# An MLP in Winograd's seven products: sums at set times, operands kept in DRAM, Silu in one step, and the last two pairs in eight products

## The chip, the cores and the metric

The kernel runs on one core of a Trainium2 chip. The metric is the device time of one execution in microseconds (us), as the median of several runs. Beside it stands one execution taken with a profile, with its own time and its span, the time from the first to the last instruction. Engines: PE is TensorE (PEld its weight loads), DVE is VectorE, ACT is ScalarE, POOL is GpSimd, SP is SyncE, which here issues the DMAs.

## The reference

The reference is one layer of a hybrid decoder trunk on x of 2048 rows by 1024 columns in float32: an RMS norm and an input projection, three mixers side by side (a diagonal state space model, a sparse attention, a gated linear recurrence), an output projection with residual, and then the part that this change is about, which ends with the final norm:

```python
h = h + mix @ w_out[l]
h = h + swiglu(rmsnorm(h, norm_ffn[l]), w_gate[l], w_up[l], w_down[l])
return rmsnorm(h, norm_final)

def swiglu(h, w_gate, w_up, w_down):
    return (jax.nn.silu(h @ w_gate) * (h @ w_up)) @ w_down
```

w_gate and w_up are 1024 by 2816, w_down is 2816 by 1024.

## The kernel before

The program has three stages. phase_a does the projections and phase_b the mixers and the output projection; it leaves the 16 tiles of 128 rows in DRAM as hS and their sums of squares in ssq. The change touches phase_c, the MLP, only.

**The MLP.** The 2048 rows are taken in two halves (s = 0 and 1) of 1024. In each half the product of weights and normalised rows is done by Winograd's form of Strassen's method: a two by two product in seven products instead of eight, with sums ahead of them and behind them. The 22 tiles of 128 columns of the hidden layer go in 11 pairs (fp). pair does, for the gate (j = 0) and the up matrix (j = 1), the seven products of a pair. Their weight operands are sums S1 to S4 of the raw weights (make, tiles "S", four buffers), split by part into a rounded high part "ah" and a low remainder "al" in float32r. Their row operands B11, B21, T2, T1, T3, B22 and T4 are 512 by 512 blocks of the rows and of differences of them, transposed by TensorE in turn4 and split into high and low as well. A product of high and low parts leaves out low by low, so each is 12 matmuls of 512 columns (4 steps of 128 by 3). The products' results are summed on VectorE and POOL to the four blocks of a pair; silu and give then make silu(gate) * up, and give writes this block and Winograd's sums of it to DRAM (gS, products 1 to 7). silu is Tanh on ScalarE and then th + 1 times g on VectorE (twice the Silu; give halves it).

**The down product.** After its 11 pairs a half does down, again by seven products, in groups of one or two pairs (GROUPS_D, six groups). fetch loads an operand pair of a product, high from gS and low from w_down or wS (its sums) through "raw", rounds it on ScalarE and takes the remainder on VectorE or POOL. block multiplies it and adds the result in PSUM (tiles "P", six banks) to one of 28 accumulators M[k, t] in SBUF, whose buffers are those of S, U2, th and other tiles of the pairs (ACC_TAGS). In the last group combine adds the accumulators up to the four blocks of the output, squares are summed on ScalarE, and finish takes a root and scales: by a VectorE step with the gain, or by a ScalarE step and a POOL multiplication. In the second half the last group has its row tile t as the outer loop, so that finish can follow each t.

**Rows and weight sums.** rows_a and rows_b make the row operands of the first half. The normalised rows of T2, T1 and T3 are made from rows loaded early into h5, l5, h6 and l6, which B22 and T4 need as their own place later; the differences overwrite the rows, so a second round of rows_b loads the rows from hS again, scales them by gain and makes the differences for B22 and T4. down_sums makes one pair's sums of w_down (wS), and ahead the second half's rows and differences (tS, four sets). Both use the tile "nx", three buffers, and "t3", one.

**The order.** Nothing here is ordered by hand on an engine. Plan records every operation with a key and, if floor is set, an earliest time, and then goes through time: a free engine takes the ready operation with the lowest key. The times of operations are the planner's own costs. What comes out is the fixed order of each engine's queue. A tile with n buffers waits for the n-th tile before it of the same name, in the order of the program:

```python
r = self.rings.setdefault(ring, [])
r.append(ref)
ref.old += r[-1 - bufs:-bufs]
```

Keys run with planned TensorE time: a product takes STEP_C, 2.724, a pair 14 of them, and the pairs of the first half end at x = 419.5. Weight parts have a key 12 ahead of their product (LEAD_W), raw weights 40, fetches of the down product 24.

## Time and profile before

| | us |
|---|---|
| median of 3 runs | 2781.14 |
| lowest and highest of them | 2781.03, 2782.69 |
| the profiled execution | 2778.5 |
| its span | 2776.7 |

| engine | busy us | share of the span |
|---|---|---|
| PE | 2577.2 | 93% |
| PEld | 2095.7 | 75% |
| DVE | 2296.8 | 83% |
| ACT | 1352.3 | 49% |
| POOL | 1376.6 | 50% |

The mean granted clock of TensorE was 0.966 of full speed. Times in the rows below count from the start of the span. phase_c lies between about 1390 us and the end. Nearly all its instructions are recorded by one helper and so carry one line, L207; they are told apart by their tiles. Busy shares are means over stages with different limits, so they are read stage by stage.

### The profile page before, as it was taken

The page shows a single profiled execution, that of the slowest core. Times are in us where ns is not written, and L with a number is a line of the kernel's source. Part 1 is how long each engine was busy: PE and PEld are TensorE (multiplying, and loading weights), DVE is VectorE, ACT ScalarE, POOL GpSimd, SP SyncE. Part 2 cuts the span into 40 slices and gives each one's busy share as a digit, 9 for nine tenths or more (in the row PEclk, how much of TensorE's full clock was granted, in tenths as well). Part 3 has the DMA queues.
Part 4 walks back from the last instruction along what each step waited for, and adds up shares of the span by engine and source line. Part 5 has one row for each costly group of instructions (what it writes and reads, how often), then busy time and mean ns, then how long its engine had stood idle before and what let it go on. Part 6 is the DMA issues. An engine that isn't in the chain of part 4 may idle for free. (4 is left out here: it accounts for less than half of the span.)

```text
span 2776.7 us, 43054 instructions
## 1 busy us (share of the span) xinstructions
PE 2577.2 (93%) x14889; PEld 2095.7 (75%) x14889; DVE 2296.8 (83%) x4480; ACT 1352.3 (49%) x2820; POOL 1376.6 (50%) x971
## 2 busy tenths in 40 slices
PE   6988889989999999998969989999998999999996
PEld 5756568777887788877758777887886888888785
DVE  8797776259898999999899999878889887877877
ACT  5662433147877777876633323344345333334433
POOL 2445441124544343443266766665466555556446
PEclk9999999979999999999989999999999999999998
DMA  5455556662212121121436665346654233326652
GB/s 170 121 157 161 148 137 199 204 171 61 70 41 64 36 64 41 41 52 41 143 105 227 242 228 198 113 145 239 214 180 148 107 107 113 104 90 235 218 200 82
DMA packets 231706, 376.11 MB, mean 135 GB/s; under 512 B 67040, under 2 KB 114912, under 8 KB 231488
## 3 DMA queue, kind: packets, MB, share of 16 engines
q1 hardware_dynamic: 185456, 339.27, 37.6%
q0 software_dynamic: 43872, 26.22, 4.7%
q10 hardware_dynamic: 2160, 7.87, 0.7%
q8 instruction: 118, 1.93, 0.3%
q14 instruction: 100, 0.82, 0.1%
HBM read 259.84 MB, written 113.44 MB: 134 GB/s over the span
## 5 line engine op out<-in xcount | busy, mean ns | idle before, releaser
L207 PE MATMUL B<-h,al 128*128 128x512 f32 x1232 | 486.7, 395 | 16.7 <-POOL al L207 11.2
L207 PE MATMUL B<-h,ah 128*128 128x512 f32 x1232 | 485.8, 395 | 16.7 <-ACT ah L207 7.1
L207 PE MATMUL B<-l,ah 128*128 128x512 f32 x1232 | 485.0, 394 | 4.5 <-DVE l L207 4.5
L207 PE MATMUL B<-l,h 128*128 128x512 f32 x1848 | 431.6, 394 | 11.7 <-POOL l L207 5.3
L207 PEld LDWEIGHTS B<-l,h 128*128 128x128 f32 x1848 | 348.0, 190 | 88.7 <-POOL l L207 8.2
L207 PEld LDWEIGHTS B<-h,al 128*128 128x128 f32 x1232 | 233.7, 190 | 72.4 <-POOL al L207 15.3
L207 PEld LDWEIGHTS B<-h,ah 128*128 128x128 f32 x1232 | 234.2, 190 | 67.0 <-ACT ah L207 8.2
L207 POOL TENSOR_TENSOR l<-raw,l 128x1024 fp32r<-128x1024 f32 (+1 forms) x84 | 195.8, 2342 | 170.2 <-ACT l L207 144.8
L207 PEld LDWEIGHTS B<-l,ah 128*128 128x128 f32 x1232 | 234.1, 190 | 54.7 <-DVE l L207 6.2
L393 DVE SCALAR_TENSOR_TENSOR ptl<-B,pth 128x512 f16<-128x512 f32 (+3 forms) x408 | 246.1, 624 | 22.4 <-ACT pth L384 21.1
L384 ACT ACTIVATE pth<-B 128x512 f16<-128x512 f32 (+3 forms) x408 | 214.4, 548 | 55.9 <-PE B L1509 31.6
L399 PE MATMUL B<-wo,mix 128*128 128x512 f32 x768 | 227.0, 412 | 4.7 <-DMA mix<-mixS 3.9
L207 ACT ACTIVATE ah<-S 128x512 fp32r<-128x512 f32 x176 | 110.4, 628 | 236.2 <-PE B L207 183.6
L207 POOL TENSOR_TENSOR U<-U,s 128x512 f32<-128x512 f32 x96 | 151.8, 1581 | 102.4 <-DVE U L207 57.3
L207 POOL TENSOR_TENSOR al<-S,ah 128x512 fp32r<-128x512 f32 x92 | 149.0, 1620 | 94.8 <-ACT ah L207 94.8
L384 ACT ACTIVATE Ps<-Ps,mn 128x1024 f32<-128x1024 f32 (+7 forms) x192 | 172.7, 902 | 41.3 <-DVE mn L1412 40.1
L399 PE MATMUL B<-KB,Q 128*128 128x384 f32 (+3 forms) x448 | 185.1, 413 | 6.4 <-DVE im L396 2.1
L207 PE MATMUL B<-hnl,wsh 128*128 128x512 f32 x448 | 183.3, 409 | 1.8 <-DVE hnl L207 1.8
L207 PE MATMUL B<-hnh,wsh 128*128 128x512 f32 x448 | 182.6, 408 | 0.5 <-ACT stage L207 0.3
L1509 PE MATMUL B<-ident,Ps 128*128 128x128 f32 x1088 | 181.1, 277 | 1.2 <-ACT Ps L384 0.8
L207 PE MATMUL B<-hnh,wsl 128*128 128x512 f32 x448 | 179.2, 400 | 0.0
L399 PE MATMUL B<-VV,ptl 128*128 128x64 f16 x1448 | 148.2, 195 | 27.8 <-DVE ptl L393 26.8
(371 smaller groups left out, 6282.1 us busy)
## 6 DMA issues: line engine op xcount, KB each, us to landing
raw<-in_wgu SPq DMA_DIRECT2D x88, 512.0 KB, 3.7
raw<-gS SPq DMA_DIRECT2D x70, 512.0 KB, 3.9
gS<-U SPq DMA_DIRECT2D x88, 256.0 KB, 2.1
raw<-wS SPq DMA_DIRECT2D x40, 512.0 KB, 4.0
gS<-s SPq DMA_DIRECT2D x66, 256.0 KB, 2.1
raw<-in_wd SPq DMA_DIRECT2D x66, 256.0 KB, 3.8
wraw<-in_wzf SPq DMA_DIRECT2D x28, 512.0 KB, 4.4
nx<-in_x SPq DMA_DIRECT2D x24, 512.0 KB, 4.5
```

Source lines behind the costliest of these rows:

```text
L207: f(*[real(x) for x in a], **{n: real(x) for n, x in k.items()})
L384: return self.S.activation(o, i, f, **k)
L393: return (eng or self.V).scalar_tensor_tensor(o, a, s, b, op0=op0, op1=op1, **k)
L399: return self.PE.matmul(o, l, r, start=start, stop=stop)
L1509: self.PE.transpose(pt.v[:, j - a], P.v[:, c:c + 128], self.ident)
```

## The change

Six things change, all in phase_c.

- **B22 and T4 by DRAM.** rows_b runs once. It stores b1 (B22) to the new uT, makes the differences for T2 and T4 together, stores b0 (T4) too, and transposes T2, T1 and T3; T3 lies in an "nx" tile. rows_c, from time 10 on, loads both blocks back and transposes them.
- **Silu.** silu is one ScalarE step with the function Silu in place; give multiplies gate and up in a plain product.
- **Earliest times.** down_sums of pair fp gets the floor 70 + 25 fp and the key 80 + 25 fp (before: 13 and 50 + 33 fp). ahead of set j gets the floor x - 190 + 25 j with x = 419.5, its key x - 150 + 25 j as before.
- **The last two pairs of the second half in eight products.** give keeps only the block itself for pairs 9 and 10 (eS) and makes no sums of it. down does five groups by seven products and combines after the fifth; ends then does, for each of the 8 row tiles and both column halves, the plain product of the last two pairs (12 matmuls each, over their four blocks of 128 hidden columns), adds it to the combined accumulator, and finish follows after the tiles two by two and one by one at the end. combine's sums into 3 go from POOL to VectorE, in both halves.
- **finish.** The first column half of the first half's tiles is scaled and multiplied by the gain in one VectorE step, instead of ScalarE and POOL; the second half's tiles, but the last, use that step for both column halves. LAST, the tiles whose gain is multiplied in before the root, is 15 alone.
- **The planner** knows Silu as a table of its own.

```diff
 GROUPS_D = (1, 2, 2, 2, 2, 2)
+TAIL = 9
...
 FIRST = ((0, 1), (1, 2), (2, 3), (3, 4))
-LAST = (11, 15)
+LAST = (15,)
...
-TABLE = {AF.Exp: 0, AF.Tanh: 0, AF.Sqrt: 1, AF.Sin: 2}
+TABLE = {AF.Exp: 0, AF.Tanh: 0, AF.Sqrt: 1, AF.Sin: 2, AF.Silu: 3}
...
         self.wS = {k: [d(f"wS{k}_{g}", [128, n, 512]) for g, n in enumerate(GROUPS_D)] for k in (4, 5, 6, 7)}
+        self.eS = d("eS", [2, 2, 128, 2, 512])
+        self.uT = [d(f"uT{j}", [2, 128, 512]) for j in range(4)]
...
                 pool.tile([128, n], F32, name=name, bufs=bufs)
-            self.recorded(pool, psum, BANKS_C, ("rstd", "ssq", "hS", "gS", "wS", "tS"), self.mlp, START_C)
+            self.recorded(pool, psum, BANKS_C, ("rstd", "ssq", "hS", "gS", "eS", "wS", "tS", "uT"), self.mlp, START_C)
...
-        def rows_b(j, names):
+        def rows_b(j):
             if j == 0:
-                for n in names:
+                for n in ("T2", "T1", "T3"):
                     operand(0, n)
-            if "T2" in names:
-                x0 = early[j // 2][:, j % 2]
-                x1 = row(4 + j, early[2 + j // 2][:, j % 2])
-                t3 = x1[:, 512:]
-            else:
-                x1, x0 = row(4 + j), row(j)
-                t3 = pool.tile([128, 512], F32, name="t3", bufs=1)
+            x0 = early[j // 2][:, j % 2]
+            x1 = row(4 + j, early[2 + j // 2][:, j % 2])
+            t3 = pool.tile([128, D], F32, name="nx", bufs=3)[:, :512]
             a0, b0, a1, b1 = x0[:, :512], x0[:, 512:], x1[:, :512], x1[:, 512:]
-            differences(a0, b0, a1, b1, t3, names)
-            src = {"T3": t3, "B22": b1, "T2": a0, "T1": a1, "T4": b0}
-            for n in names:
-                turn4(src[n], ops[0, n], 128 * j)
+            self.dma(self.uT[j][0], b1)
+            differences(a0, b0, a1, b1, t3, ("T2", "T4"))
+            self.dma(self.uT[j][1], b0)
+            for n, x in (("T2", a0), ("T1", a1), ("T3", t3)):
+                turn4(x, ops[0, n], 128 * j)
+        def rows_c(j):
+            if j == 0:
+                for n in ("B22", "T4"):
+                    operand(0, n)
+            x = pool.tile([128, D], F32, name="nx", bufs=3)
+            self.dma(x.rearrange("p (a b) -> p a b", a=2), self.uT[j].rearrange("a p b -> p a b"))
+            for i, n in enumerate(("B22", "T4")):
+                turn4(x[:, 512 * i:512 * i + 512], ops[0, n], 128 * j)
...
         def silu(g):
-            th = small("th")
-            self.act(th, g, AF.Tanh, scale=0.5)
-            self.stt(g, th, 1.0, g, OP.add, OP.mult)
+            self.act(g, g, AF.Silu)
...
             keep = lambda k, x: self.dma(self.gS[s][k][gi][:, j], x)
-            self.stt(g, g, 0.5, u, OP.mult, OP.mult)
+            self.tt(g, g, u, OP.mult)
+            if s and fp >= TAIL:
+                self.dma(self.eS[c][fp - TAIL][:, r], g)
+                return
...
-            n, first, r = GROUPS_D[gi], sum(GROUPS_D[:gi]), []
+            n, first, r = 2 if k is None else GROUPS_D[gi], sum(GROUPS_D[:gi]), []
...
                 raw = pool.tile([128, KT, 128], F32, name="raw", bufs=4).rearrange("p a b -> p (a b)")[:, :512 * n]
-                if tag == "h" or k in self.wS:
+                if k is None:
+                    src = self.eS[gi // 2][gi % 2].rearrange("p a b -> p (a b)") if tag == "h" else io["wd"][2 * TAIL + gi]
+                    self.at(x - LEAD_G, 0, self.dma, raw, src)
+                elif tag == "h" or k in self.wS:
...
                 tt(6, 1)
-                tt(3, 6, G)
+                tt(3, 6)
             elif k == 5:
-                tt(3, 5, G)
+                tt(3, 5)
...
                 tt(7, 5)
-            i = 8 * s + t
-            for i, dh, o, after in ((i, 0, 2, 2), (i, 1, 3, 3), (i + 4, 0, 4, 4), (i + 4, 1, 7, 7)):
-                if k == after:
-                    a, d = M[o, t], slice(512 * dh, 512 * dh + 512)
-                    acc[i, dh] = a
-                    junk = pool.tile([128, 512], BF, name="junk", bufs=1)
-                    self.at(x + .3, 0, lambda: self.act(junk, a, AF.Square, accum_out=ms[:, dh, col(i):col(i) + 1]))
-                    if i in LAST:
-                        if i not in last:
-                            last[i] = pool.tile([128, D], F32, name="nx", bufs=3)
-                        self.at(x + .3, 0, self.tt, last[i][:, d], a, gfin[dh], OP.mult, self.G if dh else None)
+            for i, dh, o in ((t, 0, 2), (t, 1, 3), (4 + t, 0, 4), (4 + t, 1, 7)):
+                if k == o and not s:
+                    squares(i, dh, M[o, t], x)
+        def squares(i, dh, a, x):
+            acc[i, dh], d = a, slice(512 * dh, 512 * dh + 512)
+            junk = pool.tile([128, 512], BF, name="junk", bufs=1)
+            self.at(x + .3, 0, lambda: self.act(junk, a, AF.Square, accum_out=ms[:, dh, i:i + 1]))
+            if i in LAST:
+                if i not in last:
+                    last[i] = pool.tile([128, D], F32, name="nx", bufs=3)
+                self.at(x + .3, 0, self.tt, last[i][:, d], a, gfin[dh], OP.mult)
+        def ends(i, dh, hw, x):
+            c, t = i // 4, i % 4
+            a, d = M[{(0, 0): 2, (0, 1): 3, (1, 0): 4, (1, 1): 7}[c, dh], t], slice(512 * dh, 512 * dh + 512)
+            ps = psum.tile([128, 512], F32, name="P")
+            def products():
+                for r in range(4):
+                    g, w = hw[2 * c + r // 2][0][:, :, 512 * (r % 2) + 128 * t:512 * (r % 2) + 128 * t + 128], hw[r][1][:, :, d]
+                    self.mm(ps, g[:, 0], w[:, 0], r == 0, False)
+                    self.mm(ps, g[:, 0], w[:, 1], False, False)
+                    self.mm(ps, g[:, 1], w[:, 0], False, r == 3)
+            self.at(x, 0, products)
+            self.at(x + 2.724, 0, self.tt, a, a, ps, OP.add)
+            squares(8 + i, dh, a, x + 2.724)
...
             totals(s, x)
-            for gi, n in enumerate(GROUPS_D):
-                end = gi == len(GROUPS_D) - 1
-                u = .681 * n
-                at = lambda p, t: x + u * (7 * t + p if end and s else 4 * p + t)
-                hw = {k: fetch(s, k, gi, p, at(p, 0)) for p, k in enumerate(seq)}
-                for t, p in ((t, p) for t in range(4) for p in range(7)) if end and s else ((t, p) for p in range(7) for t in range(4)):
-                    k, y = seq[p], at(p, t)
+            groups = GROUPS_D[:-1] if s else GROUPS_D
+            for gi, n in enumerate(groups):
+                u, end = .681 * n, gi == len(groups) - 1
+                hw = {k: fetch(s, k, gi, p, x + 4 * u * p) for p, k in enumerate(seq)}
+                for p, t in ((p, t) for p in range(7) for t in range(4)):
+                    k, y = seq[p], x + u * (4 * p + t)
...
                         combine(s, t, k, y + u)
-                        if s and k == 4:
-                            self.at(y + u + 1, 0, finish, 8 + t, 12 + t)
-                        elif not s and t == 3 and k in (3, 4):
+                        if not s and t == 3 and k in (3, 4):
...
                 x += 28 * u
+            if s:
+                hw = [fetch(s, None, r, r, x) for r in range(4)]
+                for i in range(8):
+                    for dh in range(2):
+                        ends(i, dh, hw, x)
+                        x += 2.724
+                    if i in (1, 3, 5):
+                        self.at(x + 1, .01, finish, 7 + i, 8 + i)
+                    elif i > 5:
+                        self.at(x + 1, 0, finish, 8 + i)
...
         M = {}
-        col = lambda i: i if i < 8 else 8 + 2 * (i % 4) + (i - 8) // 4
...
             n = len(tiles)
-            c = col(tiles[0])
+            c = tiles[0]
...
                         a = acc[i, dh]
-                        if i > 7 and dh == 0:
+                        if i > 7 or dh == 0:
...
                     self.at(x - 50 + j, 0, rows_a, j)
-                for n, names in enumerate((("T2", "T1", "T3"), ("B22", "T4"))):
-                    plan.floor = 10.0 if n else -100.0
-                    for j in range(4):
-                        self.at(x - 6 + 18 * n + 3 * j, 0, rows_b, j, names)
+                for j in range(4):
+                    self.at(x - 6 + 3 * j, 0, rows_b, j)
+                plan.floor = 10.0
+                for j in range(4):
+                    self.at(x + 12 + 3 * j, 0, rows_c, j)
...
                 if s == 0:
-                    self.at(50 + 33 * fp, 0, down_sums, fp)
+                    plan.floor = 70.0 + 25 * fp
+                    self.at(80 + 25 * fp, 0, down_sums, fp)
+                    plan.floor = REST_C
...
                 for j in range(4):
+                    plan.floor = x - 190 + 25 * j
                     self.at(x - 150 + 25 * j, 0, ahead, j)
+                plan.floor = REST_C
...
```

## Rows read from the trace of the kernel before

**Rows 1.** Windows of phase_c; columns: engines' busy us (instructions), granted clock, DMA share, GB/s

```profile
core 0: us, PE busy (x) PEld busy (x) DVE busy (x) ACT busy (x) POOL busy (x), PEclk, DMA share, GB/s
1430.00:1460.00 30.00, 19.17 (x78) 14.09 (x77) 28.60 (x31) 7.25 (x13) 17.86 (x12) 0.83 0.52 164
1570.00:1610.00 40.00, 36.59 (x160) 29.31 (x159) 36.32 (x39) 12.42 (x22) 30.19 (x20) 1.00 0.69 237
1610.00:1697.00 87.00, 76.05 (x311) 59.12 (x310) 82.15 (x80) 22.84 (x41) 58.69 (x36) 0.96 0.67 225
2080.00:2130.00 50.00, 38.53 (x176) 29.40 (x175) 46.68 (x69) 30.23 (x63) 31.01 (x21) 0.86 0.37 124
2130.00:2540.00 410.00, 410.00 (x1811) 339.45 (x1810) 325.91 (x368) 149.32 (x254) 234.28 (x156) 1.00 0.34 118
2540.00:2610.00 70.00, 66.44 (x282) 53.30 (x281) 57.33 (x68) 29.25 (x31) 38.83 (x17) 0.98 0.70 243
2710.00:2730.00 20.00, 17.06 (x63) 13.35 (x62) 14.45 (x15) 5.40 (x9) 15.38 (x10) 0.83 0.12 41
2754.80:2776.70 21.90, 0.00 (x0) 0.00 (x0) 14.79 (x26) 6.83 (x18) 10.06 (x7) 0.56 0.26 96
```

**Rows 2.** TensorE's timeline: start, us, instruction, in brackets idle before and its releaser

```profile
1446.26 0.92 PE L207 MATMUL B<-ident,nx 128*128 128x128 f32 x4 [2.54 <-DVE nx L207]
...
1452.53 0.63 PE L207 MATMUL B<-h,al 128*128 128x512 f32 x1
1452.96 0.63 PE L207 MATMUL B<-h,ah 128*128 128x512 f32 x1
...
2123.42 0.79 PE L207 MATMUL B<-h,ah 128*128 128x512 f32 x1 [4.62 <-ACT ah L207]
```

**Rows 3.** Groups of VectorE instructions from 1408 to 1456 us: busy us, mean ns

```profile
L207 DVE SCALAR_TENSOR_TENSOR nx<-nx,rstd,gain 128x1024 f32<-128x1024 f32 x8 | 13.8, 1724 | 0.0
...
L207 DVE TENSOR_TENSOR nx<-nx,t 128x512 f32<-128x512 f32 x4 | 5.9, 1483 | 0.0
L207 DVE TENSOR_TENSOR t<-nx 128x512 f32<-128x512 f32 x4 | 4.8, 1199 | 0.0
```

**Rows 4.** DMA issues of the whole span: count, KB each, median us to landing

```profile
nx<-hS SPq DMA_DIRECT2D x16, 512.0 KB, 4.5
```

**Rows 5.** Groups of instructions from 1400 to 2780 us, VectorE, POOL and ScalarE

```profile
L207 DVE SCALAR_TENSOR_TENSOR U<-th,U 128x512 f32<-128x512 f32 x44 | 51.9, 1197 | 0.6
...
L207 DVE SCALAR_TENSOR_TENSOR s<-th,s 128x512 f32<-128x512 f32 x44 | 34.9, 792 | 0.9 <-ACT th L207 0.7
...
L207 DVE SCALAR_TENSOR_TENSOR nx<-nx,rstd,gain 128x1024 f32<-128x1024 f32 x16 | 28.6, 1785 | 4.6 <-DMA nx<-hS 4.6
L207 ACT ACTIVATE th<-s 128x512 f32<-128x512 f32 x44 | 27.8, 632 | 86.7 <-DVE s L207 45.6 <-POOL s L207 41.1
...
L207 DVE TENSOR_TENSOR nx<-nx,t 128x512 f32<-128x512 f32 x19 | 21.5, 1134 | 5.5 <-POOL nx L207 5.5
...
L207 DVE TENSOR_TENSOR t<-nx 128x512 f32<-128x512 f32 x19 | 18.0, 945 | 0.3
...
L207 POOL TENSOR_TENSOR th<-th,ah 128x512 f32<-128x512 f32 x8 | 11.3, 1406 | 0.8 <-DVE ms L207 0.6
```

**Rows 6.** Windows of one pair each, with Wd sums beside it and without

```profile
1500.10:1538.30 38.20, 38.20 (x170) 31.62 (x170) 36.75 (x38) 12.66 (x22) 28.93 (x18) 1.00 0.64 221
2314.40:2352.50 38.10, 38.10 (x169) 31.53 (x168) 30.16 (x34) 13.11 (x22) 21.07 (x15) 1.00 0.30 105
```

**Rows 7.** SP's timeline, the first and the last of 22 loads of w_down for sums

```profile
1441.90 5.90 SPq L207 DMA_DIRECT2D nx<-in_wd  x2
...
1606.06 0.33 SPq L207 DMA_DIRECT2D nx<-in_wd  x1
```

**Rows 8.** VectorE's timeline: a row set's gain, the second half's S1, the last accumulation

```profile
1629.03 1.28 DVE L207 SCALAR_TENSOR_TENSOR nx<-nx,rstd,gain 128x1024 f32<-128x1024 f32 x1 [2.12 <-DMA nx<-hS]
...
2107.54 0.68 DVE L207 TENSOR_TENSOR S<-raw 128x512 f32<-128x512 f32 x1
...
2766.61 0.68 DVE L207 TENSOR_TENSOR gain<-gain,B 128x512 f32<-128x512 f32 x1
```

## The prediction

> **What bounds the kernel now.** I read the windows by stage first, then in each stage with an idle TensorE the timeline of the engine it waited for. Up to 1380 us nothing is touched by the diff, so only the last stage counts, the MLP from about 1390 us. There TensorE is the bound: between 2130 and 2540 us it is busy all 410 us, 1811 instructions, 0.226 us each [rows 1]. Time can be won only where it stands still or runs slow. The stretches are [rows 1]: 1430 to 1460, idle 30 − 19.2 = 10.8 us; 1570 to 1697, idle 3.4 + 11.0 = 14.4; the turn from the first half to the second, 2080 to 2130, idle 11.5; 2540 to 2610, idle 3.6; 2710 to 2730, idle 2.9; and the tail, 21.9 us with no product at all. After such a pause the granted clock is at its lower level: matmuls then start 0.43 us apart instead of 0.23 [rows 2], 0.2 us lost on each. Counting these in the timeline I put it at about 12 products in the first stretch (2.4 us), 13 in the second (2.6), 23 at the turn (4.6), 7 (1.4) and 15 (3.0). So the prizes are about 13, 17, 16, 5, 6 and 22 us.
>
> What ends the first wait is VectorE's "nx" [rows 2]: it is working through the second round of row sums. What ends those of 1570 to 1697 is mostly the low parts "al", late because VectorE (82 of 87 us busy) and POOL carry row sums and Wd sums beside the pairs [rows 1]. At the turn ScalarE's "ah" ends the longest wait, 4.6 us [rows 2], because S was late on VectorE.
>
> **1. B22 and T4 by DRAM.** Before, rows_b's second round spent on VectorE 8 gains of 1.72 us, 4 of 1.48 and 4 of 1.20, 24.5 us out of the 48 from 1408 to 1456 [rows 3]. All of it goes: b1 and b0 are written once and read back. Added are 8 stores and 4 loads on SP; a 512 KB load of "nx" lands in 4.5 us [rows 4], the stores are half its size and bounded by the same 4.5. Written by about 1410, they are back by about 1425, before B22 and T4 are due near 1430. The four POOL subtractions for T4 come earlier, at about 1.4 us each [rows 5], beside the first T2 sums, on a VectorE that is full there. That may delay the first products: 0 to 4 us, I take 1.5, since POOL has idle time there. Of the 13 us I take 12; bounds 8 and 13.
>
> **2. Silu in one step.** Four scalar_tensor_tensor per pair leave VectorE; over both halves 51.9 + 34.9 = 86.8 us [rows 5]. A quiet pair holds 30.2 us of VectorE in 38.1 [rows 6]; four silus of it are 4 × 0.99 = 3.9 us, so 26.2 remain. The gain itself hides behind TensorE where nothing waits; it pays only through the next item. ScalarE does Silu where it did Tanh; no row has a Silu. The nearest, Tanh, is 0.63 us [rows 5]; above, ScalarE has 38.1 − 13.1 = 25 us free per pair [rows 6], 6.2 per silu, so up to 6.9 us each it costs nothing. I take nothing.
>
> **3. Earliest times for the sums.** Before, the 11 Wd sums ran from 1442 to 1606 [rows 7], one each 15 us, raising a pair's VectorE from 30.2 to 36.8 us and POOL's from 21.1 to 28.9 [rows 6]; then four row sets in 90 us, where TensorE lost most. One Wd sum costs VectorE 0.95 + 1.13 = 2.1 us, a row set 2 × 1.79 + 2.1 = 5.7 [rows 5]. With one sum per 25 us a pair holds 26.2 + 1.5 × 2.1 = 29.4 us, less than a quiet pair of before, which never stalls. So the waits around 1570 to 1625 go.
> The row sets are another matter. Their floors say 229 + 25j on the planner's clock, but "nx" has three buffers handed on in program order, and the eleventh Wd sum comes first with floor 320. So the sets cannot finish before about 330. By then their keys (269 to 344) lie behind the clock and make them urgent. I expect them between about 1712 and 1790 us, packed: 50 to 60 us for 4 × 5.7 = 22.6 us of VectorE on top of 26.2 per 38.1. That is 57 us of work in 50 or 64 in 60, an overshoot of 4 to 7 us. It meets a VectorE that comes in with slack and parts made 12 us ahead, where before it came in already late. I take 4 us lost here against 17, a gain of 13; bounds 2 (the same crowd, later) and 17.
>
> **4. The turn.** The finish of the first half puts dh 0 on VectorE in one step, and the sums of products 6 and 5 into 3 move there: 16 operations from POOL at about 1.41 us [rows 5]. For: S tiles are accumulators, and the next half's S1 waits until they are written out; it began at 2107.5 [rows 8], after ScalarE, POOL and a store for each. One VectorE step in place of two should free them some 4 to 5 us sooner. Against: VectorE is 46.7 of 50 us busy there [rows 1], and 16 more operations at 0.68 to 1.4 us are 11 to 22 us, with POOL's 22 us gone that now stretch its operations. I take a gain of 5 out of 16; bounds 16 and a loss of 8.
> The Trainium skill (SBUF — State Buffer, Who interferes with whom) says that a VectorE instruction with two SBUF inputs and a GpSimd one that reads SBUF exclude each other for a whole instruction. By it the moved work would cost VectorE 16 × 0.68 and give back about as much waiting, so the turn would gain some 10 us and the sum below would be 5 us lower; no row of before shows this stretch without POOL.
>
> **5. The last two pairs by eight products.** TensorE gets 16 × 12 = 192 products for 7 × 4 × 6 = 168: 24 × 0.226 = +5.4 us, all on the path; bounds 5.4 and, at the lower clock, 10. The fetches fall from 14 buffers to 8 and start when the group before frees its first four positions, 16 us ahead, so the wait at 2710 to 2730 goes; against that, eight combinations more on VectorE during that group: I count 28 additions of 0.68 [rows 8], 20 combinations near 1.13 [rows 5] and 4 splits of double width, 1.4 to 2.3 by the same two, some 49 us of VectorE in its 38, which the six banks and the following 44 us of light work must absorb. Of 6 us I take 4; bounds 6 and a loss of 5. The pairs 9 and 10 skip three POOL sums, one VectorE sum and three stores each: 1.5 of the 5 us near 2550; bounds 0 and 5.
> The tail: products end at 2754.8, but VectorE's last accumulation starts at 2766.6 [rows 8], 11.8 us late behind combinations and finishes. After the change each tile takes TensorE 5.4 us and VectorE about 4 (two additions of 0.68, two scalings of 0.68 to 1.1, half a root), so no backlog. From that addition to the end it was 2776.7 − 2766.6 = 10.1 us with three squares after it and four stores; two squares less at 0.63 (Tanh as the nearest row [rows 5]) and two issues less at 0.33 [rows 7] leave 8.1. So 21.9 becomes 8, a gain of 14; bounds 8 and 15.
>
> **Sum.** 1.5 − 12 − 13 − 5 + 5.4 − 4 − 1.5 − 14 = −42.6. The profiled execution took 2778.5 us (span 2776.7), so 2735.9; the timed runs' median, 2781.1, lies 2.6 above it: **2738 us**.
>
> **Rivals.** (a) The late row sets stall TensorE as the early ones did: item 3 gives 2, not 13: 2749. For it: keys behind the clock, and before 82 us of VectorE work came with 76 us of products [rows 1]. Against: VectorE is 4 us per pair lighter.
> (b) The turn gets worse: 16 operations in a full engine cost 8 instead of winning 5: 2751. Against it: POOL's stretching goes with them.
> (c) The last group stalls on banks because VectorE lags 10 us there: +5 for −4: 2747.
> (d) Slower: a floor pins a sum's place in VectorE's in-order queue near when the planner thinks its load has landed; if the load is late, all behind it waits. It was so at 1629, 2.1 us [rows 8]. There are 11 + 8 + 4 such loads; to turn 42 us of gain, each must hold VectorE 1.9 us beyond the 12 us lead. From 2.2 us each the kernel is slower, about 2788. Against: DMA is lighter when spread, and only two such waits on row loads stood in the timeline before.
> (e) The change does not do what it says: sums were never what held TensorE, and the waits come back as port contention from POOL; only the tail and the 5.4 remain, with the turn worse by 8: 2781 − 14 + 5 + 8 = 2780.
>
> **How the numbers follow.** Forecast 0.56, (a) 0.14, (b) 0.12, (c) 0.06, (d) 0.06, (e) 0.06. The forecast's own range is 2724 to 2745, from item 4's ends (2727 with its 16) and the small bounds. With (a) to (c) the range is 2720 to 2756, leaving (d), (e) and the edges outside. A measurement of this kernel tells about 0.2%, 5.6 us, from no change. Faster: the first four cases, 0.88; same 0.06 from (e); slower 0.06 from (d).
>
> **What would show it.** No TensorE wait on "nx" near 1430 to 1460, and no VectorE gain steps there; a quiet pair at about 26 us of VectorE; Wd sums some 25 us apart to about 1710; row sets after them, not among them; S1 of the second half earlier against the last product; eight products a tile to the end and a tail near 8 us. Wrong if TensorE waits on "al" from 1710 to 1800 for over 8 us, if the turn's idle time is over 16 us, or if the tail stays over 14.

## The result and the profile after

The changed kernel takes **2763.5 us** (median of four runs, 2759.1 to 2766.2) against 2781.3: ratio 0.9933, 95% interval 0.9916 to 0.9951. It is 18 us faster; I had forecast 43 and a range of 2720 to 2756. The profiled execution took 2759.1 us, its span 2757.3.

TensorE's timeline cuts the MLP into stages, each from its first product to that of the next; the last is what follows the last product. Lengths in us, with the forecast put together from the prediction's items:

| stage | before | after | change | forecast |
|---|---|---|---|---|
| pairs 1 (first half) | 474.6 | 443.2 | -31.4 | 1.5 - 12 - 13 = -23.5 |
| down 1 | 226.1 | 240.3 | +14.2 | 0 |
| pairs 2, with the turn | 438.9 | 434.3 | -4.6 | -5 |
| down 2 | 222.3 | 239.6 | +17.3 | 5.4 - 4 - 1.5 = -0.1 |
| tail | 21.9 | 8.5 | -13.4 | -14 |
| sum | 1383.8 | 1365.9 | -17.9 | -42.6 |

Turn and tail came within 1 us of the forecast, the first pairs 8 better. The two down products lost 31.5 us. Windows of the kernel before for three of these stages (columns as in [rows 1]):

```profile
1392.90:1867.50 474.60, 443.82 (x1929) 359.31 (x1930) 428.93 (x463) 154.16 (x269) 313.80 (x200) 0.97 0.53 179
1867.50:2093.60 226.10, 220.87 (x1006) 181.00 (x1005) 188.86 (x230) 101.67 (x137) 129.75 (x63) 1.00 0.62 209
...
2532.50:2754.80 222.30, 215.78 (x925) 175.86 (x923) 182.00 (x219) 92.31 (x114) 130.01 (x62) 0.98 0.56 193
...
```

Of the changed kernel, the same stages and the tail, then windows that answer to [rows 1] and a quiet pair that answers to [rows 6]:

```profile
1391.40:1834.60 443.20, 433.54 (x1929) 357.68 (x1930) 363.07 (x402) 156.33 (x269) 300.57 (x198) 0.98 0.55 191
1834.60:2074.90 240.30, 226.79 (x1006) 184.82 (x1005) 196.90 (x239) 101.62 (x136) 124.64 (x56) 0.97 0.59 199
...
2509.20:2748.80 239.60, 224.61 (x949) 180.51 (x948) 183.51 (x238) 86.92 (x115) 105.64 (x47) 0.96 0.47 166
2748.80:2757.30 8.50, 0.00 (x0) 0.00 (x0) 3.96 (x11) 1.65 (x4) 0.00 (x0) 0.68 0.33 123
...
1430.00:1460.00 30.00, 30.00 (x138) 24.94 (x138) 24.63 (x34) 11.57 (x21) 19.73 (x14) 1.00 0.41 135
...
1610.00:1697.00 87.00, 87.00 (x386) 72.06 (x385) 70.57 (x78) 29.63 (x50) 58.37 (x39) 1.00 0.57 197
...
2610.00:2710.00 100.00, 87.22 (x350) 68.38 (x350) 78.66 (x89) 29.18 (x30) 56.85 (x24) 0.91 0.39 136
...
2314.40:2352.50 38.10, 38.10 (x170) 31.56 (x169) 27.02 (x32) 13.23 (x22) 20.74 (x14) 1.00 0.31 104
...
```

A stage's length less its PE busy time is TensorE's idle time; PE busy at the same count of instructions shows the clock. Down 1 has 1006 instructions in both kernels: idle 5.2 became 13.5 (+8.3), busy 220.9 became 226.8 (+5.9: the granted clock is 0.97 over the stage instead of 1.00, with products at the lower level after the waits). Down 2: idle 6.5 became 15.0 (+8.5), and its 24 products more cost 5.4 by the prediction's price, so 3.4 of the 8.8 more busy time is clock. Pairs 1 won 21.1 of idle time and 10.3 of clock on the same 1929 instructions.

TensorE's timeline shows where down 2 stands still: in its fifth group, where combine now lies. Three of seven waits, 12.6 us together:

```profile
2668.99 2.18 PE L208 MATMUL B<-l,h 128*128 128x512 f32 x6 [2.81 <-DVE ah L208]
...
2676.41 2.90 PE L208 MATMUL B<-l,h 128*128 128x512 f32 x6 [1.12 <-DVE ah L208]
...
2702.75 2.47 PE L208 MATMUL B<-l,h 128*128 128x512 f32 x5 [6.18 <-DVE th L208]
```

Down 1 stands still in three places: 6.7 us at 1842 and 1860, behind VectorE's "U", 2.1 at 1904, behind POOL's "l" (the kernel before has 1.9 in that group), and 4.0 at 2043 in its last group, which combines too:

```profile
1842.01 11.86 PE L208 MATMUL B<-l,h 128*128 128x512 f32 x51 [2.51 <-DVE U L208]
...
1860.35 41.84 PE L208 MATMUL B<-l,h 128*128 128x512 f32 x175 [4.21 <-DVE U L208]
1904.29 0.97 PE L208 MATMUL B<-l,h 128*128 128x512 f32 x3 [2.10 <-POOL l L208]
...
2043.10 1.62 PE L208 MATMUL B<-l,h 128*128 128x512 f32 x3 [3.95 <-DVE l L208]
```

The timeline of all engines before the wait at 1860, and a window of the 8 us before it:

```profile
1848.60 0.43 SPq L208 DMA_DIRECT2D raw<-wS  x1
...
1855.13 1.06 ACT L208 ACTIVATE l<-raw 128x1024 fp32r<-128x1024 f32 x1 [6.62 <-DMA raw<-wS]
...
1856.40 1.06 ACT L208 ACTIVATE h<-raw 128x1024 fp32r<-128x1024 f32 x1 [0.20 <-DMA raw<-gS]
...
1857.49 2.21 DVE L208 TENSOR_TENSOR h<-raw,h 128x1024 fp32r<-128x1024 f32 x1 [2.90 <-ACT h L208]
1859.63 0.67 DVE L208 TENSOR_TENSOR U<-U,B 128x512 f32<-128x512 f32 x1
...
1860.35 1.17 PE L208 MATMUL B<-l,h 128*128 128x512 f32 x3 [4.21 <-DVE U L208]
...
1848.00:1856.00 8.00, 8.00 (x40) 6.52 (x38) 6.53 (x8) 1.38 (x3) 1.18 (x1) 1.00 1.01 335
```

ScalarE stands 6.6 us before a fetch that was issued at 1848.60, and 0.2 us more before the next one; VectorE's low part waits for ScalarE's high part, and behind it in VectorE's queue stands the accumulation that frees a PSUM bank. ScalarE and POOL are nearly idle, but the DMA engines are full (share 1.01): from these lines alone it can be the full DMA engines or the order in which fetches and steps stand in the queues. The last group of runs comes back to this.

### The profile page after: what moved, and what is told of

The parts are those of the page before. It is cut to its first block, busy times and chain, and to the rows that moved or that the text cites. A ratio compares the mean times of both kernels' runs of the same rounds, so it can differ in the third digit from the quotient of the medians.

```text
span 2757.3 us, 42980 instructions
## 1 busy us (share of the span) xinstructions
PE 2578.8 (94%) x14913; PEld 2102.5 (76%) x14913; DVE 2191.3 (79%) x4396; ACT 1340.4 (49%) x2801; POOL 1306.3 (47%) x930
## 4 chain that ended last, share of the span: by engine, by line
PE 56%; DVE 23%; DMA 8%; issue 5%; POOL 4%; ACT 3%; SPq 1%; POOLq 0%; DVEq 0%; ACTq 0%
PE B L208 42%; PE B L402 10%; DVE l L208 4%; PE B L1512 3%; DVE ptl L396 3%; DVE Ps L1415 3%; DMA raw<-wS 2%; POOL l L208 2%; DMA raw<-gS 1%; DVE acc L396 1%; DMA l<-kcS 1%; DVE h L208 1%; SPq L208 1%; DVE s L208 1%; DVE al L208 1%
## 5 line engine op out<-in xcount | busy, mean ns | idle before, releaser
L208 PE MATMUL B<-l,h 128*128 128x512 f32 x1872 | 445.5, 398 | 28.1 <-DVE U L208 7.1
L208 PEld LDWEIGHTS B<-l,h 128*128 128x128 f32 x1872 | 355.9, 192 | 110.7 <-issue 12.7
L387 ACT ACTIVATE pth<-B 128x512 f16<-128x512 f32 (+3 forms) x408 | 214.5, 549 | 55.8 <-PE B L1512 31.5
L402 PE MATMUL B<-wo,mix 128*128 128x512 f32 x768 | 226.8, 411 | 5.1 <-DMA mix<-mixS 4.4
L208 POOL TENSOR_TENSOR U<-U,s 128x512 f32<-128x512 f32 x92 | 143.5, 1560 | 111.1 <-DVE s L208 55.1
L208 POOL TENSOR_TENSOR al<-S,ah 128x512 fp32r<-128x512 f32 x92 | 140.6, 1530 | 97.7 <-ACT ah L208 95.6
L208 DVE TENSOR_TENSOR h<-raw,h 128x1024 fp32r<-128x1024 f32 (+1 forms) x81 | 125.1, 1545 | 65.8 <-ACT h L208 65.6
```

Source lines behind the costliest of these rows:

```text
L208: f(*[real(x) for x in a], **{n: real(x) for n, x in k.items()})
L387: return self.S.activation(o, i, f, **k)
L402: return self.PE.matmul(o, l, r, start=start, stop=stop)
```

## The experiments

Each ratio is to the kernel before on the same chip; stage lengths are from the profiled execution. Down 1 has nearly the changed kernel's order in pool3_half2 and low_vector too and took 242.8 and 242.2 there, so under 3 us in one stage says nothing.

| run | ratio (95%) | pairs 1 | down 1 | pairs 2 | down 2 | tail |
|---|---|---|---|---|---|---|
| changed kernel | 0.9933 (0.9916-0.9951) | 443.2 | 240.3 | 434.3 | 239.6 | 8.5 |
| only_dram | 0.9975 (0.9966-0.9983) | 469.5 | 227.1 | 439.3 | 225.2 | 21.6 |
| only_floors | 0.9990 (0.9981-0.9998) | 467.9 | 232.9 | 440.3 | 223.8 | 22.0 |
| only_silu | 1.0027 (1.0017-1.0036) | 469.2 | 235.2 | 439.0 | 227.9 | 21.7 |
| only_eight | 0.9988 (0.9979-0.9997) | 479.3 | 228.2 | 438.7 | 232.4 | 8.2 |
| pool3_half2 | 0.9918 (0.9903-0.9934) | 443.6 | 242.8 | 434.5 | 235.2 | 8.5 |
| pool3_half1 | 0.9898 (0.9882-0.9914) | 443.6 | 236.2 | 430.2 | 240.4 | 8.5 |
| low_vector | 0.9900 (0.9884-0.9916) | 443.5 | 242.2 | 434.6 | 231.4 | 8.5 |
| finish_pool | 0.9944 (0.9924-0.9963) | 445.4 | 240.6 | 439.3 | 239.5 | 8.6 |
| sets_early | 0.9925 (0.9913-0.9937) | 446.1 | 238.4 | 435.7 | 241.0 | 8.9 |
| silu_back | 0.9932 (0.9919-0.9945) | 456.6 | 235.9 | 431.4 | 233.3 | 8.9 |
| three | 0.9858 (0.9846-0.9871) | 443.5 | 233.8 | 430.2 | 229.8 | 9.0 |
| three_sums7 | 0.9869 (0.9854-0.9883) | 446.0 | 233.6 | 430.2 | 230.2 | 8.6 |
| four | 0.9843 (0.9830-0.9857) | 446.4 | 229.5 | 430.2 | 230.2 | 8.5 |
| no_residual | 0.9884 (0.9871-0.9898) | 443.8 | 238.0 | 432.8 | 234.1 | 8.5 |
| new_order | 0.9833 (0.9819-0.9846) | 444.3 | 228.5 | 430.0 | 230.1 | 9.0 |
| price_low | 0.9913 (0.9898-0.9928) | 444.8 | 241.4 | 435.7 | 227.9 | 8.9 |
| before_price | 0.9983 (0.9974-0.9992) | 479.0 | 225.0 | 437.9 | 219.9 | 18.0 |
| four_price | 0.9812 (0.9797-0.9826) | 443.1 | 225.0 | 432.0 | 227.3 | 8.6 |

**The last groups and the turn.** combine's sums into 3 back on POOL, in one half each; the low parts of Wd in the fifth group of the second half on VectorE; the first half's finish on ScalarE and POOL:

```diff
-                tt(3, 6)        # and tt(3, 5)
+                tt(3, 6, G if s else None)        # pool3_half2; pool3_half1: if not s
...
-                self.at(x - LEAD_D, 0, self.tt, v[:, 1], raw, v[:, 0].bitcast(F32), OP.subtract, self.V if tag == "h" else self.G)
+                self.at(x - LEAD_D, 0, self.tt, v[:, 1], raw, v[:, 0].bitcast(F32), OP.subtract,
+                        self.V if tag == "h" or s and gi == 4 and k else self.G)        # low_vector
...
-                        if i > 7 or dh == 0:
+                        if i > 7:        # finish_pool
```

> The sums of products 6 and 5 into 3 go back to POOL, in the second half only. Theory: in the changed kernel these 8 sums stand in VectorE's queue of the fifth group, take 2.2 to 2.9 us beside POOL's low parts and hold up the additions that free the PSUM banks; TensorE then idles 12.8 us between 2660 and 2710. Back on POOL, that idle time falls under 5 us and the time by 8 to 12, to 2751 to 2755. Rival: the group stalls because sums stand beside fetches at all, whichever engine has them; then POOL delivers low parts late, TensorE waits for l or h for 8 us or more, and the time stays within 4 us of the changed kernel's 2763.

> The same in the first half only. Theory: the last group of the first down product loses less idle time (now 4.0 us at 2043 and a low clock after it), worth 4 to 6; the turn, where POOL has work again, may give 0 to 4 of it back: 2757 to 2763. Rival: these sums were hidden and their move is what shortened the turn: 3 to 8 slower, 2766 to 2771.

> In the fifth group of the second half POOL's seven low parts of Wd go to VectorE, which so has 7 more operations of double width; nothing else is moved. Theory that POOL's running operation makes VectorE's wait: the sums and accumulations fall from 2.2 to 2.9 us to about 0.7, which gives back more than the seven cost, the idle time at 2660 to 2710 falls under 5 us and the time by 6 to 10. Rival, VectorE is simply overloaded there: it gets 8 to 10 us more of work, the idle time grows, and the time rises by 4 to 10.

> The first column half of the first half's tiles is finished by ScalarE and POOL again, as before. Theory (prediction's step 4): the S tiles come free later and the turn loses 4 to 6 us: 2767 to 2769. Rival: the turn's gain came from the two sums moved off POOL or from lighter products, and the time does not change by more than 2.

With the sums on POOL, down 2 fell by 4.4, not 8 to 12: the waits on VectorE went, but four on POOL's l came (7.7 us), so each theory had half. low_vector takes 8.2 off down 2 although VectorE has more to do. Groups of the fifth group, 2655 to 2710, in the changed kernel (count | busy us, mean ns | idle before):

```profile
L208 POOL TENSOR_TENSOR l<-raw,l 128x1024 fp32r<-128x1024 f32 x9 | 24.4, 2722 | 10.2 <-ACT l L208 10.2
...
L208 DVE TENSOR_TENSOR U<-U,al 128x512 f32<-128x512 f32 x4 | 7.4, 1845 | 0.0
L208 DVE TENSOR_TENSOR th<-th,ah 128x512 f32<-128x512 f32 x4 | 6.5, 1618 | 0.0
L208 DVE TENSOR_TENSOR s<-s,al 128x512 f32<-128x512 f32 x4 | 5.5, 1378 | 0.0
...
L208 DVE TENSOR_TENSOR al<-al,B 128x512 f32<-128x512 f32 x6 | 4.0, 675 | 0.0
```

and of the same stretch of low_vector, 2662 to 2717:

```profile
L208 POOL TENSOR_TENSOR l<-raw,l 128x1024 fp32r<-128x1024 f32 x4 | 11.6, 2908 | 12.9 <-ACT l L208 12.9
...
L208 DVE TENSOR_TENSOR s<-s,al 128x512 f32<-128x512 f32 x4 | 6.0, 1504 | 0.0
...
L208 DVE TENSOR_TENSOR al<-al,B 128x512 f32<-128x512 f32 x6 | 4.0, 674 | 0.0
...
L208 DVE TENSOR_TENSOR th<-th,ah 128x512 f32<-128x512 f32 x4 | 2.7, 680 | 0.0
L208 DVE TENSOR_TENSOR U<-U,al 128x512 f32<-128x512 f32 x4 | 2.7, 678 | 0.0
```

Here "th" and "U" hold the accumulators of 3, so these eight are the sums that the change moved. They fall from 13.9 to 5.4 us when POOL's low parts are gone; the sums into "s" stay slow, beside POOL's other sums; additions with a PSUM input take 0.67 us in both. So the sums do stretch beside POOL. That this is what the 8.2 us paid for is not shown, since low_vector also has another order of the queues. Two runs below speak against it as the whole cause: silu_back, where the down products have the changed kernel's code, and price_low, the changed kernel with a new order and nothing else. Windows of the fifth group, from its first product to the first of the eight products, in the changed kernel, silu_back and price_low:

```profile
2645.90:2702.70 56.80, 44.06 (x170) 32.80 (x168) 50.87 (x52) 14.39 (x14) 37.05 (x18) 0.89 0.37 125
2663.90:2709.20 45.30, 40.74 (x170) 32.34 (x169) 44.76 (x45) 13.46 (x13) 33.09 (x15) 0.96 0.39 126
2656.70:2701.70 45.00, 40.75 (x170) 33.21 (x169) 43.81 (x43) 11.88 (x12) 29.31 (x15) 0.92 0.35 108
```

and groups of silu_back, 2664 to 2719:

```profile
L208 POOL TENSOR_TENSOR l<-raw,l 128x1024 fp32r<-128x1024 f32 x8 | 22.1, 2778 | 7.2 <-ACT l L208 7.2
...
L208 DVE TENSOR_TENSOR U<-U,al 128x512 f32<-128x512 f32 x4 | 9.3, 2316 | 0.0
...
L208 DVE TENSOR_TENSOR th<-th,ah 128x512 f32<-128x512 f32 x4 | 4.8, 1202 | 0.0
```

In silu_back the eight sums take 14.1 us beside POOL's low parts, as long as in the changed kernel, and yet the group is 11.5 us shorter, with 4.6 us of idle time for 12.7. VectorE is busy for 44.8 of its 45.3 us, and for 43.8 of 45.0 in price_low. So there are two losses in this group: in these two orders it takes about 7 us more than its products' 38.1, with VectorE busy nearly throughout, and the changed kernel's order adds 11 to 12 to that.

In the first half the sums on POOL took 4.1 off down 1 and 4.1 off pairs 2, so on VectorE they seem to cost the turn something; but new_order below has them on VectorE and the same 430 us in pairs 2. finish_pool made pairs 2 5.0 longer and changed little else: the step in finish is the whole gain of the turn in this order.

**Single parts on the kernel before.** Their edits are the change's own, one at a time.

> The kernel before with B22 and T4 by DRAM alone. Prediction's item 1: the wait on nx near 1446 and its slow products go, at 0 to 4 us for POOL's subtractions: 8 to 12 faster, ratio 0.9957 to 0.9971. Rival: with silu still in two steps VectorE is so full from 1408 to 1460 that a wait on al takes the place of that on nx: at most 4 faster.

> The kernel before with the earliest times alone. Theory: the waits of 1570 to 1697 came from sums and row sets in the same pairs; spread out they mostly go, but the sets now end shortly before the down product and slow its first 70 us: 4 to 10 faster, ratio 0.9964 to 0.9986. Rival: VectorE has no room without the lighter silu, and the waits only move: within 3 of before.

> The kernel before with silu in one ScalarE step alone. Prediction's item 2: nothing by itself, within 3 of before. Rival: the waits of 1570 to 1697 end when VectorE delivers, and 3.9 us less of VectorE work in each pair shortens them directly: 5 to 12 faster, ratio 0.9957 to 0.9982.

> The kernel before with the eight products for the last two pairs alone, with their sums into 3 on VectorE in the second half; the first half is as before. Prediction's item 5: 14 faster, ratio 0.995. Theory now: the tail gives 13, but the group with the combinations loses 12 to 17 where I had a gain of 4, and the products cost 5.4: within 5 of before, ratio 0.998 to 1.002.

only_dram gave 7 us, between theory and rival: the waits on nx went, but waits on al of 6.0 us in all came 96 to 144 us into the stage. only_silu is slower by 0.27%: it wins 5 in pairs 1 and loses 9 in down 1 and 6 in down 2. only_eight lies in the range of the new theory, but not as it said: the tail gave 13.7, down 2 lost 10.1, which is 4.7 beyond the 5.4 of its products and not 12 to 17, and the first pairs, which no edit of this run touches, took 4.8 more. The four change pairs 1 by -5.1, -6.7, -5.4 and +4.8; together they took off 31.4. I read this as an overload of VectorE that goes only when all of it goes; the runs show that the parts do not add, and not why.

**Late row sets, silu, and edits together.**

```diff
-                    plan.floor = 70.0 + 25 * fp
-                    self.at(80 + 25 * fp, 0, down_sums, fp)
+                    plan.floor = 70.0 + 16 * fp
+                    self.at(80 + 16 * fp, 0, down_sums, fp)        # sets_early
```

silu_back undoes silu and give's plain product. three is sets_early, pool3_half1 and low_vector; three_sums7 also gives (7, 6) and (7, 5) to POOL in the second half; four is three with VectorE's low parts in both halves' last groups.

> The changed kernel with the sums of w_down 16 apart instead of 25 (first floor and key as they are), so that the last is due at 230 and the row sets can run at their own floors of 229 to 304. Theory: in the changed kernel the sets wait for the last sum in the ring of nx, come packed up to 1795 us, and their stores and the next half's loads crowd the start of the first down product; its first 70 us lose 8.8 us of waits and 4 to 5 of clock, and the pairs 3.2. Undone, 6 to 12 faster than the changed kernel: ratio to before 0.989 to 0.991. Rival: sums 16 apart bring back the stalls that the kernel before had around 1570 to 1697, since VectorE then has sums and sets at once: no change or up to 6 slower, 0.993 to 0.9955.

> The changed kernel with silu in two steps again. Theory (prediction's items 2 and 3): with 3.9 us more for VectorE in each pair the sums and sets no longer fit and the waits on al come back in the first half's pairs: 8 to 15 slower than the changed kernel, ratio 0.996 to 0.999. Rival, from the run of silu alone, which was slower by 0.27%: the one-step silu costs in the down products as much as it gives in the pairs: within 3 of the changed kernel or faster, 0.990 to 0.9945.

> The changed kernel with three edits: sums 16 apart, the first half's sums into 3 on POOL, and the fifth group's low parts of Wd on VectorE in the second half. Theory, the three lie in different stretches and add: 6 to 12, 8 and 8 faster than the changed kernel, 2732 to 2742, ratio 0.983 to 0.987. Rival: each is mostly a different order of the queues and they don't add: 2750 to 2756, ratio 0.989 to 0.991.

> As the run before, and in the second half the sums with product 7 (7 + 6, 4 + 7, 7 + 5) all on POOL, which has nothing to do in the eight products' 46 us, where tiles 4 and 7 are needed only after half of it. Theory that VectorE's backlog in the fifth group is what is left there (the wait of 4.8 us on th with low parts on VectorE): 3 to 6 faster than the run before. Rival: POOL's sums make VectorE's steps wait for them as the low parts did: within 2 of it or slower.

> As the run with three edits, and the low parts of Wd in the first half's last group on VectorE too. Theory that POOL's low parts and sums together are what is late there (waits of 2.0 and 2.4 us on l): 3 to 6 faster than the run with three. Rival: VectorE then has too much at the end of the first down product and at the turn: no change or up to 5 slower.

My theory of the late sets fell: done earlier, their waits on al move to 264 to 346 us into the stage and the total stays. silu_back ties with the changed kernel: 13 worse in pairs 1, but down 1, down 2 and pairs 2 win 4, 6 and 3. three added up (0.0035 + 0.0033 + 0.0008 off 0.9933 is 0.9857) and lies in the range of ratios that I had given. three_sums7 gave nothing more, but shows what fills the fifth group: with eight sums less VectorE is busy for 36.4 us there instead of 44.8, and the group takes 38.7 where it took 45.8 in three. The waits came back among the eight products, 51.7 us for 45.9:

```profile
2646.60:2685.30 38.70, 38.42 (x169) 31.47 (x169) 36.41 (x49) 13.10 (x14) 19.71 (x9) 1.00 0.48 158
2685.30:2737.00 51.70, 47.47 (x193) 38.01 (x191) 26.77 (x58) 14.27 (x37) 17.35 (x12) 0.93 0.17 62
```

four took 4 more off down 1.

**The order of the queues.** The planner's price of a VectorE step, in the MLP alone:

```diff
-        return .07 + n * (DVE / 2 if one and not psum else DVE), None, None
+        return (.09 if self.start is START_C else .07) + n * (DVE / 2 if one and not psum else DVE), None, None        # price_low: .05
```

before_price is this edit in the kernel before; four_price is four without sets_early, with this edit. no_residual loads no h into the accumulators and so leaves the residual out.

> The changed kernel with the planner's price of a VectorE step in the MLP 0.02 us higher: the same work, in another order of the queues. Theory that a down product's length hangs on the order in which its fetches, sums and accumulations stand in the queues: each of the four stages changes by 2 to 8 us, the down products most, and the total by up to 8 either way. Rival: the lengths come from the work itself: each stage within 2 us of the changed kernel and the total within 3.

> The changed kernel without the 32 loads of h into the accumulators and the 8 subtractions for them; the first accumulation is a copy by VectorE, so the residual is left out of the output. This takes 4 MB of loads from the start of each down product. Theory that fetches land late there because the DMA engines are full (share 0.97 at 1840 to 1860): the first 70 us of the first down product lose under 3 us of waits where they lost 8.8, and the stage falls by 6 to 10; the second down product falls by 1 to 3. Rival, ScalarE's and VectorE's queue order and the four buffers of raw are what makes them late: the waits on U and l stay, within 3 us.

> The kernel before with the planner's price of a VectorE step in the MLP 0.02 us higher, nothing else. Theory that the changed kernel had an unlucky order and the kernel before an ordinary one: within 6 us of before, ratio 0.998 to 1.002, its down products within 3 of 226 and 222. Rival, the price is too low in any case and a higher one makes every order better: 10 to 25 faster, ratio 0.991 to 0.9965.

> The changed kernel with the price 0.02 us lower. Theory that lengths scatter with the order: the down products take 228 to 242, the total is anywhere from 2741 to 2768. Rival, too low a price is what costs: as slow as the changed kernel or slower, down products 240 or more, 2763 to 2785.

> The changed kernel with the higher price, the first half's sums into 3 on POOL, and the low parts of Wd of the last group by seven products on VectorE in both halves. Theory that the order and the last groups' contention are separate losses: 5 to 12 faster than the higher price alone (2741), 2729 to 2736, ratio 0.979 to 0.9815. Rival, the order had already taken them away: within 4 of 2741.

new_order issues the same operations and is about 28 us faster than the changed kernel by the ratios (0.0100 of 2781; 24 us by the stages of the two profiles). I had said up to 8 either way, so even the theory was far too small. Its down products, and those of four_price below them:

```profile
1842.90:2071.40 228.50, 221.84 (x997) 181.34 (x996) 190.93 (x235) 100.07 (x132) 119.01 (x56) 0.99 0.65 208
...
2501.50:2731.50 230.00, 220.44 (x949) 179.67 (x947) 187.22 (x236) 86.12 (x114) 107.69 (x47) 0.99 0.52 173
...
```

```profile
1840.70:2065.70 225.00, 220.44 (x1006) 181.17 (x1005) 192.60 (x238) 101.88 (x136) 113.90 (x57) 1.00 0.65 212
...
2497.70:2725.00 227.30, 220.98 (x949) 180.28 (x947) 182.40 (x243) 86.14 (x113) 91.62 (x40) 0.98 0.51 174
...
```

The order took 11.8 us off down 1 (less than 1 of it by short transposes that now stand behind it, in pairs 2), 9.5 off down 2 and 4.3 off pairs 2, with most of the low clock gone as well. No one price is right: in the kernel before the higher one gives 0.17%, and in the changed kernel the lower one leaves down 1 at 241 and brings down 2 to 228. Windows of down 1's first group in the changed kernel, new_order and no_residual:

```profile
1834.60:1863.10 28.50, 21.68 (x94) 16.94 (x93) 22.83 (x24) 14.71 (x23) 19.19 (x11) 0.96 0.88 303
1842.90:1864.00 21.10, 20.24 (x88) 15.66 (x87) 17.32 (x20) 11.85 (x21) 15.88 (x10) 1.00 0.93 324
1842.40:1863.10 20.70, 19.34 (x86) 15.59 (x84) 19.30 (x22) 13.25 (x21) 14.86 (x10) 1.00 0.84 278
```

Without the 4 MB of loads at each start (no_residual) the idle time of this group falls from 6.8 to 1.4 us, but other waits come after it: 5.3 us in the first 70, where I had said under 3, and the stage falls by only 2.3, down 2 by 5.5. The planner wrote a new order here too, so this run does not part the loads from the order. new_order does better: its DMA engines are no less full in this group (share 0.93 for 0.88), and TensorE idles 0.9 us. Full DMA engines alone do not make the wait. four_price, at 2732.1 us (2728.3 to 2736.1), is the fastest run here, and its down 1 is back under the 226 of before.

## Why the prediction was wrong

- **Items 1 and 3, pairs 1: right, and too small by 8.** No wait on nx, sums 25 us apart, a quiet pair at 27.0 us of VectorE where I said 26, 3.2 us of waits at the row sets where I said 4. The term that was mis-sized is the clock: I counted 5 us of slow products, it was 10.3, which is 5.3 of the 8. only_dram and only_floors show that the parts do not have these prices one by one.
- **Item 2, silu as nothing by itself: wrong.** A step is 0.63 us on ScalarE, as Tanh was, but alone it lengthens both down products. They hold no silu at all; what the edit can change there is the order, and when the buffers of "th", which accumulators use too, come free. The runs do not part the two.
- **Item 4, the turn: -4.6 for -5, but not as written.** The finish gives 5; pool3_half1 says that the moved sums take 4 from it, and 4 more in down 1, which I had not costed. By the Trainium skill (SBUF — State Buffer, Who interferes with whom) I had weighed a gain of 10. The exclusion itself agrees with the trace (1845 ns beside POOL, 678 without). The gain of 10 by it did not come in the changed kernel's order; new_order, with the same work, has 8.9, so the order decides here too.
- **Item 5, the last group: the step that failed.** I had some 49 us of VectorE work in 38 and let "the six banks and the following 44 us of light work" absorb it. The work was about as counted (VectorE is busy for 50.9 us there, for 44 to 45 in silu_back and price_low), but it was not absorbed: sums stand in VectorE's queue ahead of the accumulations that free the banks, and in better orders the group still takes 45 us for 38. The changed kernel's order makes it 56.8. Instead of winning 4 the stage lost 8.5 of idle time and 3.4 of clock. Rival (c) named place and cause and gave it 9; down 2 came out 17 worse than forecast, and 6 worse in price_low's order. The tail came as forecast.
- **Down 1: the term that was missing.** I took it as untouched because its code is, but for the sums into 3. The order written by the planner is not: the same work takes 228.5 or 241. The last group may add to it: pool3_half1 takes 4.1 off, and four another 4.3 from three, but these edits write a new order as well.

The sum missed 24.7 us: 31.6 on the two down products and 1.0 on turn and tail, less the 7.9 that pairs 1 gave more. That the order costs so much is shown by new_order; which exchange of places costs what is not: the chain at 1860 was read, not undone. None of the three signs that were to show me wrong came (3.2 us of waits at the row sets, 6.5 of idle time at the turn, a tail of 8.5): all three watch stages that came out right, and none watches a down product. In new_order's order the sum would have come out (its stages give -41.9 for -42.6), but by luck: pairs and turn 10.7 better than forecast, down products and tail 11.4 worse.

## What to carry to other kernels

Where a planner writes the queues, every edit writes them all anew: time the change with one or two neutral prices before you judge it, and put that scatter (here 28 us; 5 us in the kernel before) into the range. Where an edit moves one engine's work into a stretch, set its sum there against TensorE's time: 44 us of VectorE's work made a group of 38 us into one of 45 even in its better orders. A run that changes one thing in the program also changes the order, so by itself it does not price that thing. A wait of 2 to 6 us of TensorE is worth more than its length: down 1 paid 8.3 us of waits with 5.9 of low clock.

## What the hardware showed that I had not expected

A VectorE sum of two SBUF tiles takes 0.68 us by itself and 1.6 to 1.85 (mean) beside POOL's low parts, while one with a PSUM input keeps its 0.67. That stretching alone did not set a stage's length: the same eight sums took 13.9 us in a group of 56.8 and 14.1 in one of 45.3. Silu costs one table load of 1.28 us, at 1423.6, that the kernel before does not have in phase_c, and there is none after it until the root's at 2717.7, though squares and copies follow.
